# A QKV projection on one core: x's first row tiles spread over two DMA queues and handled in pairs

## The chip, the cores and the metric

The kernel runs on one core of a Trainium2 chip. The metric is the device time of one execution in microseconds. A core has TensorE (matmuls; the profile's PE, its weight loads PEld), VectorE (DVE), ScalarE (ACT), GpSimd (POOL) and SyncE (SP), which run their own instruction streams and wait for each other through semaphores. SP, ScalarE and GpSimd also issue DMAs; all of them run on the core's 16 DMA engines.

## The reference

```python
x:     16 x 512 x 768, fp32      w_qkv: 768 x 2304, fp32
qkv = np.matmul(x, w_qkv)
q, k, v = the three blocks of 768 columns
return np.stack([q, k, v], axis=0)
```

It is one matrix product of 8192 rows of x by 2304 columns, with 768 to sum over, whose columns are stored as three arrays.

## The kernel before, in words

The rows of x are taken in 32 pairs of two row tiles of 128 rows. The 768 values that are summed over are six k-slices of 128: slice j holds the rows p*6 + j of w. The columns of w are two blocks of 1024 (q = 0 and 1), each of two halves of 512 (c = 0 and 1), and a remainder of 256 columns.

Pairs 2 and up are computed with seven block products for each block of columns instead of eight, after Strassen and Winograd (`product`, `do`, lines 240 to 289), for which sums of blocks of x (`sums_x`) and of w (`sum_w`, L120) are needed. Pairs 0 and 1, the first four row tiles, are computed directly (`block`, L487): they need only casts to bf16, so that TensorE can work while w still arrives. All is in an order written out by hand, and each engine keeps the order of the program.

The head of the kernel, which the change touches, goes like this:

- **Loads.** On SP's queue: x's row tile 0, then tiles 1 to 3 (`load_row`, L169; 384 KB each, rows of 3 KB), then w slice by slice (`load_w`, L93): the first k-slice of the first 512 columns in two halves of 256 columns, then five slices of 256 KB, then six slices of the second 512 columns, then pair 2 of x in eight parts (L138) and larger blocks of w. On ScalarE's queue: two "touches", 128 bytes from each of 128 rows of w (L431) and of x's row tile 2 (L432); nothing reads them. Loads from SP and ScalarE take eight semaphores in turn, so each waits until the eighth load before it has landed.
- **GpSimd's queue.** A one-column copy of a slice of w (`hold`, L445) makes GpSimd wait until the sixth slice has landed; then it issues the DMAs of w's remainder (L450), and then it holds again, for pair 2 of x.
- **Row tiles.** Each row tile is cast to bf16, its first 384 columns by VectorE and the other 384 by ScalarE (`cast_row`, by `copy_halves`, L172 and L173). TensorE turns it with six 128x128 transposes (`turn_row`, L190) into two PSUM tiles of three. VectorE copies one of them to SBUF and ScalarE the other (L172, L173 again, with bf16 in PSUM as input). The program goes tile by tile: cast tile 0, turn tile 0, copy tile 0, cast tile 1, and so on, with the copy of a tile behind the cast of the next from tile 2 on.
- **Dummies.** `busy(n)` (L458) has TensorE multiply zeros, 8 times at the start and 2, 2 and 1 times between the transposes.
- **Casts of w.** `cast_j` casts a slice of w to bf16, on VectorE (L465) or ScalarE (L463).
- **First products.** `block` goes through the k-slices in order and adds each to the four row tiles' sums: for slice 0 the low 256 columns of tiles 0 to 2, their high 256 columns, and then tile 3 whole; then slices 1 to 5, four tiles each. A second call does the same for the second 512 columns, where the last three slices are taken tile by tile. Then come the remainder's products for those tiles (L334), and the products of pair 2.

`first`, the list of groups for slice 0, is this:

```python
    lo, hi = slice(0, half), slice(half, CB)
    first = [((0, ), range(3), lo), ((0, ), range(3), hi), ((0, ), (3, ))]
    first += [((j, ), range(4)) for j in range(1, KT)]
```

Code printed by the profile's line numbers:

Of the kernel before, what the change touches and what calls it, by code (L numbers as in the profile page):

```python
# [10 lines left out]
def kernel(  # L11
# [20 lines left out]
    nc = tc.nc  # L32
    P = 128
    G = 32
    B, T, H = x.shape
    M = B * T
    K = H
    N3 = w_qkv.shape[1]
    KT = K // P
    KH = KT // 2  # L40
# [3 lines left out]
    REM = N3 - 4 * CB  # L44
    Q_OFF = (0, 2 * CB + REM)
    R_OFF = 2 * CB
    fp32 = mybir.dt.float32
    f32r = mybir.dt.float32r
    bf16 = mybir.dt.bfloat16
# [4 lines left out]
    x_flat = x.rearrange("b t h -> (b t) h")  # L54
# [15 lines left out]
    m_pool = ctx.enter_context(tc.tile_pool(name="m", bufs=2))  # L70
    ps_pool = ctx.enter_context(tc.tile_pool(name="ps", bufs=8, space=bass.MemoryType.PSUM))
# [4 lines left out]
    eye = w_pool.tile([P, 176], bf16, name="eye")[:, :P]  # L76
    w_rem = [w_pool.tile([P, KH, REM], bf16, name="w_rem0"), None]

    b1 = [w_pool.tile([P, KT, CB], bf16, name=f"b1_{q}") for q in range(2)]
# [11 lines left out]
    def load_w(dst, j0, nj, off, cols):  # L91
        rows = w_qkv.rearrange("(p j) n -> p j n", j=KT)
        nc.sync.dma_start(dst, rows[:, j0:j0 + nj, off:off + cols])  # L93

    stage = {}
# [7 lines left out]
    def load_blocks(q, c):  # L103
        for h in range(2):
            if c == 0 and h == 0:
                t = st_first
            else:
                t = st_pool.tile([P, KH, CB], fp32, name="st1", tag="st")[:]
            load_w(t, h * KH, KH, Q_OFF[q] + c * CB, CB)
            stage[q, h, c] = t  # L110
# [11 lines left out]
    xin, xf, xb, sr = {}, {}, {}, {}  # L122
# [39 lines left out]

    def load_row(p, r):
        if r == 0:
            xin[p] = xin_pool.tile([P, 2, K], fp32, name="xin")
        row = (2 * p + r) * P
        nc.sync.dma_start(xin[p][:, r], x_flat[row:row + P, :])  # L169

    def copy_halves(dst, src):
        nc.vector.tensor_copy(out=dst[0], in_=src[0])  # L172
        nc.scalar.activation(dst[1], src[1], ident)  # L173
# [3 lines left out]
    def cast_row(p, r):  # L177
        if r == 0:
            xc[p] = s_pool.tile([P, 2, K], bf16, name="xc", tag="s")
        halves = (slice(0, K // 2), slice(K // 2, K))  # L180
        copy_halves([xc[p][:, r, n] for n in halves], [xin[p][:, r, n] for n in halves])

    def turn_row(p, r):
        if r == 0:
            xb[p] = xb_pool.tile([P, KT, 2 * P], bf16, name="xb", tag="xb")
        cols = xc[p][:, r, :].rearrange("m (p j) -> m j p", j=KT)
        ks = (slice(0, KH), slice(KH, KT))
        ps = [ps_pool.tile([P, KH, P], bf16, name="ps") for _ in ks]
        for j in range(KT):
            nc.tensor.transpose(ps[j // KH][:, j % KH, :], cols[:, j, :], eye)  # L190
        return lambda: copy_halves(
            [xb[p][:, n, r * P:(r + 1) * P] for n in ks], [t[:] for t in ps]
        )
# [6 lines left out]
    act, dve = nc.scalar, nc.vector  # L200
# [55 lines left out]
    def bank():  # L256
        return ps_pool.tile([P, CB], fp32, name="ps")
# [168 lines left out]
    ND = 2  # L426
    zero = xb_pool.tile([P, CB], bf16, name="zero", tag="xb")
    nc.vector.memset(zero[:], 0.0)
    load_row(0, 0)
    touch = m_pool.tile([P, 2, G], fp32, name="touch")  # L430
    nc.scalar.dma_start(touch[:, 0], w_qkv.rearrange("(p j) n -> p j n", j=KT)[:, 0, :G])  # L431
    nc.scalar.dma_start(touch[:, 1], x_flat[2 * P:3 * P, :G])  # L432
    nc.scalar.activation(tiny[:], zero[:, :1], ident)
    make_identity(nc, eye)
    load_row(0, 1)
    load_row(1, 0)
    load_row(1, 1)
    half = CB // 2
    load_slices(0, [(0, 1, 0, half), (0, 1, half, CB)] + [(j, 1, 0, CB) for j in range(1, KT)])
    load_slices(1, [(j, 1, 0, CB) for j in range(KT)])  # L440
# [2 lines left out]
    def hold(src):  # L443
        mark = m_pool.tile([P, 1], fp32, name="mark")
        nc.gpsimd.tensor_copy(out=mark[:], in_=src)  # L445

    hold(stage[0, 1, 0][:, KH - 1, :1])
    for h in range(2):
        rows = w_qkv.rearrange("(p j) n -> p j n", j=KT)[:, h * KH:(h + 1) * KH]
        nc.gpsimd.dma_start(w_rem[h][:], rows[:, :, R_OFF:R_OFF + REM])  # L450
    hold(xin[2][:, 0, :1])
    load_blocks(1, 0)

    def busy(n):

        ps = bank()
        for _ in range(n):
            nc.tensor.matmul(ps[:], zero[:, :P], zero[:], start=True, stop=True)  # L458

    def cast_j(q, c, w, j, eng=act, n=slice(0, CB)):  # L460
        src = stage[q, j // KH, c][:, j % KH, n]
        if eng is act:
            eng.activation(w[:, j, n], src, ident)  # L463
        else:
            eng.tensor_copy(out=w[:, j, n], in_=src)  # L465
# [54 lines left out]
        sums_x(p)  # L520

    lo, hi = slice(0, half), slice(half, CB)
    first = [((0, ), range(3), lo), ((0, ), range(3), hi), ((0, ), (3, ))]
    first += [((j, ), range(4)) for j in range(1, KT)]

    busy(8)
    cast_row(0, 0)
    turned = [turn_row(0, 0)]
    busy(2)
    turned[0]()  # L530
    cast_row(0, 1)
    turned.append(turn_row(0, 1))
    busy(2)
    cast_row(1, 0)
    turned[1]()
    turned.append(turn_row(1, 0))
    busy(1)
    cast_row(1, 1)
    turned[2]()
    cast_j(0, 0, b1[0], 0, dve, lo)  # L540
    turned.append(turn_row(1, 1))
    cast_j(0, 0, b1[0], 0, dve, hi)
    turned[3]()
    for j in range(1, KT):
        cast_j(0, 0, b1[0], j, dve)
    late0 = block(0, 0, b1[0], first)
# [165 lines left out]
```

## Time and profile before

| | |
|---|---|
| median of 3 runs | 360.48 us (360.26 to 360.60) |
| the profiled execution | 360.26 us |
| its span in the profile | 358.5 us |
| TensorE busy | 351.8 us (98%), 1760 instructions |
| VectorE, ScalarE, GpSimd busy | 65%, 52%, 50% |
| DMA | 107.73 MB, mean 301 GB/s over the span |

The span runs from the core's first instruction to its last; what lies around it, 1.76 us, is start and end of the execution. Times inside it count from the span's start. A matmul's end is modelled: the distance between the starts of two matmuls in a row is what one of them costs, 0.22 us for 512 columns when TensorE runs at its pace. In a row of the timeline, the figures are start, duration, engine, line, operation, output and input with shapes, and a count where several instructions in a row were merged; in brackets is the idle time before it and what ended it. "DMA to landing" counts from the start of the issue to the last semaphore update.

### The profile page before, as it was taken

The page shows a single profiled execution, that of the slowest core. Times are in us where ns is not written, and L with a number is a line of the kernel's source. Part 1 is how long each engine was busy: PE and PEld are TensorE (multiplying, and loading weights), DVE is VectorE, ACT ScalarE, POOL GpSimd, SP SyncE. Part 2 cuts the span into 40 slices and gives each one's busy share as a digit, 9 for nine tenths or more (in the row PEclk, how much of TensorE's full clock was granted, in tenths as well). Part 3 has the DMA queues.
Part 4 walks back from the last instruction along what each step waited for, and adds up shares of the span by engine and source line. Part 5 has one row for each costly group of instructions (what it writes and reads, how often), then busy time and mean ns, then how long its engine had stood idle before and what let it go on. Part 6 is the DMA issues. An engine that isn't in the chain of part 4 may idle for free.

```text
span 358.5 us, 5212 instructions
## 1 busy us (share of the span) xinstructions
PE 351.8 (98%) x1760; PEld 252.6 (70%) x1780; DVE 231.7 (65%) x245; ACT 185.5 (52%) x316; POOL 178.5 (50%) x187
## 2 busy tenths in 40 slices
PE   8999999999999999999999999999999999999995
PEld 4465577767768687786867768687776867768764
DVE  3789776878475675746676474676647577544643
ACT  5469644445545545454554545545454544545443
POOL 0223775582664717447372664717447371754420
PEclk9999999999999999999999999999999999999999
DMA  7998999999999898989989799898989989755767
GB/s 265 347 373 313 323 353 360 369 346 342 339 298 317 286 261 328 261 317 299 289 323 250 309 283 332 282 264 329 268 293 307 294 321 251 312 217 224 273 243 256
DMA packets 82106, 107.73 MB, mean 301 GB/s; under 512 B 5408, under 2 KB 62240, under 8 KB 82080
## 3 DMA queue, kind: packets, MB, share of 16 engines
q1 hardware_dynamic: 74288, 101.86, 86.1%
q10 hardware_dynamic: 6992, 5.15, 5.9%
q0 software_dynamic: 800, 0.39, 0.8%
q8 instruction: 14, 0.23, 0.3%
q14 instruction: 12, 0.10, 0.1%
HBM read 32.28 MB, written 75.50 MB: 301 GB/s over the span
## 4 chain that ended last, share of the span: by engine, by line
PE 93%; DMA 4%; ACT 1%; ACTq 1%; issue 0%
PE ps L251 78%; PE ps L306 11%; PE ps L487 4%; DMA st<-in_w_qkv_dram 3%; DMA touch<-in_x_dram 1%; PE ps L334 1%; ACT o L286 0%; ACTq L385 0%; ACT orem L399 0%; ACT both L463 0%; ACTq L431 0%; ACTq L401 0%; ACTq L399 0%
## 5 line engine op out<-in xcount | busy, mean ns | idle before, releaser
L251 PE MATMUL ps<-t,s 128*128 128x512 f32 x720 | 178.5, 396 | 0.0
L251 PEld LDWEIGHTS ps<-t,s 128*128 128x128 f32 x720 | 134.9, 188 | 29.8 <-ACT o L276 0.3
L154 DVE STREAM_TRANSPOSE xf<-xin 128x1536 f32<-128x1536 f32 (+1 forms) x33 | 91.2, 2767 | 2.5 <-DMA xin<-in_x_dram 2.5
L218 POOL TENSOR_TENSOR s<-xf 128x384 fp32r<-128x384 f32 x29 | 30.8, 1061 | 116.4 <-PE ps L251 115.0
L251 PE MATMUL ps<-b,xb 128*128 128x512 bf16 x342 | 81.7, 379 | 1.2
L283 DVE TENSOR_TENSOR o<-o,ps 128x512 f32<-128x512 f32 x58 | 39.7, 685 | 60.2 <-ACT o L282 60.2
L251 PEld LDWEIGHTS <-xb 128*128 128x128 bf16 x360 | 33.8, 98 | 36.9 <-issue 4.7
L273 DVE TENSOR_TENSOR o<-o,ps 128x512 f32<-128x512 f32 x60 | 39.0, 681 | 29.5 <-PE ps L251 22.4
L282 ACT ACTIVATE o<-ps 128x512 f32<-128x512 f32 x58 | 34.7, 598 | 44.2 <-PE ps L251 44.2
L276 ACT ACTIVATE o<-ps 128x512 f32<-128x512 f32 x60 | 36.0, 600 | 36.6 <-PE ps L251 34.0
L289 DVE TENSOR_TENSOR o<-o,ps 128x512 f32<-128x512 f32 x60 | 41.1, 687 | 20.7 <-PE ps L251 19.6
L260 ACT ACTIVATE o<-ps 128x512 f32<-128x512 f32 x60 | 35.7, 597 | 31.3 <-PE ps L251 18.3
L251 PE MATMUL ps<-b,s 128*128 128x512 f32 x180 | 50.4, 389 | 0.0
L198 POOL CAST xb<-xf 128x1536 bf16<-128x1536 f32 x28 | 41.0, 1464 | 16.7 <-DVE xf L154 16.7
L286 ACT ACTIVATE o<-ps 128x512 f32<-128x512 f32 x60 | 35.9, 598 | 24.3 <-PE ps L251 21.3
L306 PE MATMUL ps<-w_rem,xb 128*128 128x256 bf16 x360 | 44.6, 273 | 0.0
L306 PEld LDWEIGHTS <-xb 128*128 128x128 bf16 x360 | 34.9, 98 | 11.0 <-issue 1.1
L251 PEld LDWEIGHTS ps<-b,s 128*128 128x128 f32 x180 | 33.8, 188 | 7.1
L219 POOL TENSOR_TENSOR s<-s,xf 128x384 fp32r<-128x384 f32 x29 | 29.3, 1009 | 1.3
L220 POOL TENSOR_TENSOR s<-xf 128x384 fp32r<-128x384 f32 x29 | 29.3, 1009 | 0.0
L222 POOL TENSOR_TENSOR s<-xf,s 128x384 fp32r<-128x384 f32 x29 | 29.3, 1009 | 0.0
L323 ACT ACTIVATE orem<-ps 128x512 f32<-128x512 f32 x31 | 18.5, 597 | 20.7 <-PE ps L306 10.9
(47 smaller groups left out, 127.4 us busy)
## 6 DMA issues: line engine op xcount, KB each, us to landing
out_dram<-o SPq DMA_DIRECT2D x62, 768.0 KB, 4.5
xin<-in_x_dram SPq DMA_DIRECT2D x90, 192.0 KB, 6.5
out_dram<-o SPq DMA_DIRECT2D x65, 256.0 KB, 3.7
out_dram<-orem SPq DMA_DIRECT2D x31, 256.0 KB, 5.5
xin<-in_x_dram ACTq DMA_DIRECT2D x22, 192.0 KB, 6.9
st<-in_w_qkv_dram SPq DMA_DIRECT2D x11, 256.0 KB, 5.2
st<-in_w_qkv_dram SPq DMA_DIRECT2D x3, 768.0 KB, 10.0
xin<-in_x_dram SPq DMA_DIRECT2D x4, 384.0 KB, 4.5
```

The lines of the kernel that those rows point to most:

```text
L154: lambda g=g: nc.vector.transpose(turned[:, g:g + n], rows[:, g:g + n])
L198: nc.gpsimd.tensor_copy(out=xb[p][:], in_=t[:])
L218: 1: lambda g: g.tensor_tensor(s[:, 1], a21, a22, op=add),
L251: nc.tensor.matmul(ps[:], lhs[j], rhs[j], start=(start and j == 0), stop=(j == KH - 1), skip_group_check=True,)
L260: nc.scalar.activation(u.o[:, 0, :CB], u.x[:], ident)
L273: nc.vector.tensor_tensor(c11, c11, u.z[:], op=add)
L276: nc.scalar.activation(c12, u.x[:], ident)
L282: nc.scalar.activation(c22, u.x[:], ident)
L283: nc.vector.tensor_tensor(c22, c22, u.y[:], op=add)
L286: nc.scalar.activation(c21, u.x[:], ident)
L289: nc.vector.tensor_tensor(c12, c12, u.y[:], op=add)
L306: nc.tensor.matmul(ps, xb[p][:, j, r * P:(r + 1) * P], w_rem[j // KH][:, j % KH, :], start=(j == 0), stop=(j == KT - 1), skip_group_check= ...
```

## The change

1. x's row tiles 1 and 3 are loaded by ScalarE's queue instead of SP's, behind the touch of w. The touch of x is gone. SP's queue has tiles 0 and 2 and then w, as before.
2. The casts divide 448 columns to VectorE and 320 to ScalarE. The transposes go to PSUM tiles of four and two slices; VectorE copies the four, ScalarE the two.
3. The four tiles go in pairs: both casts of tiles 0 and 1, then all twelve transposes, then both copies; then the same for tiles 2 and 3. The dummies are 8 at the start and 2 behind the first twelve transposes.
4. Slice 0 of w: VectorE casts the low 256 columns, GpSimd the high 256. This cast stands ahead of GpSimd's first hold.
5. Slice 0 in `block`: low columns of tiles 0 and 1, high columns of tiles 0 and 1, then tiles 2 and 3 whole.

```diff
-    def load_row(p, r):
+    def load_row(p, r, eng=nc.sync):
...
-        nc.sync.dma_start(xin[p][:, r], x_flat[row:row + P, :])
+        eng.dma_start(xin[p][:, r], x_flat[row:row + P, :])
...
-        halves = (slice(0, K // 2), slice(K // 2, K))
+        halves = (slice(0, K * 7 // 12), slice(K * 7 // 12, K))
...
-        ks = (slice(0, KH), slice(KH, KT))
-        ps = [ps_pool.tile([P, KH, P], bf16, name="ps") for _ in ks]
-        for j in range(KT):
-            nc.tensor.transpose(ps[j // KH][:, j % KH, :], cols[:, j, :], eye)
+        ks = (slice(0, KT - 2), slice(KT - 2, KT))
+        ps = [ps_pool.tile([P, n.stop - n.start, P], bf16, name="ps") for n in ks]
+        for n, t in zip(ks, ps):
+            for j in range(n.start, n.stop):
+                nc.tensor.transpose(t[:, j - n.start, :], cols[:, j, :], eye)
...
-    load_row(0, 0)
-    touch = m_pool.tile([P, 2, G], fp32, name="touch")
-    nc.scalar.dma_start(touch[:, 0], w_qkv.rearrange("(p j) n -> p j n", j=KT)[:, 0, :G])
-    nc.scalar.dma_start(touch[:, 1], x_flat[2 * P:3 * P, :G])
+    touch = m_pool.tile([P, G], fp32, name="touch")
+    nc.scalar.dma_start(touch[:], w_qkv.rearrange("(p j) n -> p j n", j=KT)[:, 0, :G])
+    for p in range(2):
+        load_row(p, 0)
+        load_row(p, 1, nc.scalar)
     nc.scalar.activation(tiny[:], zero[:, :1], ident)
     make_identity(nc, eye)
-    load_row(0, 1)
-    load_row(1, 0)
-    load_row(1, 1)
...
-    first = [((0, ), range(3), lo), ((0, ), range(3), hi), ((0, ), (3, ))]
+    first = [((0, ), range(2), lo), ((0, ), range(2), hi), ((0, ), range(2, 4))]
...
     busy(8)
-    cast_row(0, 0)
-    turned = [turn_row(0, 0)]
+    for r in range(2):
+        cast_row(0, r)
+    turned = [turn_row(0, r) for r in range(2)]
     busy(2)
-    turned[0]()
-    cast_row(0, 1)
-    turned.append(turn_row(0, 1))
-    busy(2)
-    cast_row(1, 0)
-    turned[1]()
-    turned.append(turn_row(1, 0))
-    busy(1)
-    cast_row(1, 1)
-    turned[2]()
+    for f in turned:
+        f()
+    for r in range(2):
+        cast_row(1, r)
     cast_j(0, 0, b1[0], 0, dve, lo)
-    turned.append(turn_row(1, 1))
-    cast_j(0, 0, b1[0], 0, dve, hi)
-    turned[3]()
+    cast_j(0, 0, b1[0], 0, nc.gpsimd, hi)
+    hold(stage[0, 1, 0][:, KH - 1, :1])
...
+    hold(xin[2][:, 0, :1])
+    load_blocks(1, 0)
+    for r in range(2):
+        turn_row(1, r)()
```

The lines with the holds, w's remainder and `load_blocks(1, 0)` are moved down unchanged; SP issues the same DMAs behind the row tiles in the same order.

More of the change, by code (lines that the diff above doesn't have):

```diff
@@ L445, in hold @@
         nc.gpsimd.tensor_copy(out=mark[:], in_=src)
[L447 to L452, printed above, removed]
     def busy(n):
@@ L522 @@
     lo, hi = slice(0, half), slice(half, CB)
-    first = [((0, ), range(3), lo), ((0, ), range(3), hi), ((0, ), (3, ))]
+    first = [((0, ), range(2), lo), ((0, ), range(2), hi), ((0, ), range(2, 4))]
     first += [((j, ), range(4)) for j in range(1, KT)]
     busy(8)
-    cast_row(0, 0)
-    turned = [turn_row(0, 0)]
+    for r in range(2):
+        cast_row(0, r)
+    turned = [turn_row(0, r) for r in range(2)]
     busy(2)
-    turned[0]()
-    cast_row(0, 1)
-    turned.append(turn_row(0, 1))
-    busy(2)
-    cast_row(1, 0)
-    turned[1]()
-    turned.append(turn_row(1, 0))
-    busy(1)
-    cast_row(1, 1)
-    turned[2]()
-    cast_j(0, 0, b1[0], 0, dve, lo)
-    turned.append(turn_row(1, 1))
-    cast_j(0, 0, b1[0], 0, dve, hi)
-    turned[3]()
+    for f in turned:
+        f()
+    for r in range(2):
+        cast_row(1, r)
+    cast_j(0, 0, b1[0], 0, dve, lo)
+    cast_j(0, 0, b1[0], 0, nc.gpsimd, hi)
+    hold(stage[0, 1, 0][:, KH - 1, :1])
+    for h in range(2):
+        rows = w_qkv.rearrange("(p j) n -> p j n", j=KT)[:, h * KH:(h + 1) * KH]
+        nc.gpsimd.dma_start(w_rem[h][:], rows[:, :, R_OFF:R_OFF + REM])
+    hold(xin[2][:, 0, :1])
+    load_blocks(1, 0)
+    for r in range(2):
+        turn_row(1, r)()
     for j in range(1, KT):
```

## The prediction

> **What bounds the kernel now.** I read the page's first two parts and its chain, then the chain of waits in order of time, the timeline of the first 20 us by engine, the stretches of half a microsecond, and the DMA view of single stretches. The chain by engine (page), then its start in order of time (start, us, what):
>
> ```profile
> PE 93%; DMA 4%; ACT 1%; ACTq 1%; issue 0%
> ```
> ```profile
> 1.18 4.04 DMA touch<-in_x_dram
> ...
> 5.23 5.24 DMA st<-in_w_qkv_dram
> ...
> 10.48 6.09 DMA st<-in_w_qkv_dram
> ...
> 16.60 0.64 ACT both L463
> ...
> 17.28 2.32 PE ps L487 x10
> ```
>
> Up to 16.6 us the end is set by transfers, from 17.28 us to the last stores by TensorE without a real gap. So only the head can change, and a shift of TensorE's work there goes through to the end one for one. The last link of the head is the last 256 KB slice of w: it lands at 10.48 + 6.09 = 16.57, ScalarE casts it, TensorE takes it at 17.28. The timeline shows how close the race is (start, us, engine, line, operation; a release in brackets):
>
> ```profile
> 4.08 0.52 ACT L173 ACTIVATE xc<-xin 128x384 bf16<-128x384 f32 x1 [0.92 <-DMA xin<-in_x_dram]
> 6.49 0.84 PE L190 MATMUL ps<-eye,xc 128*128 128x128 bf16 x6
> 6.72 0.36 DVE L172 CAST xc<-xin 128x384 bf16<-128x384 f32 x1 [0.89 <-DMA xin<-in_x_dram]
> 7.60 0.50 PE L190 MATMUL ps<-eye,xc 128*128 128x128 bf16 x6
> 7.88 0.36 DVE L172 CAST xc<-xin 128x384 bf16<-128x384 f32 x1 [0.47 <-DMA xin<-in_x_dram]
> 8.46 0.54 PE L190 MATMUL ps<-eye,xc 128*128 128x128 bf16 x6
> 8.83 5.36 PE L487 MATMUL ps<-b,xb 128*128 128x256 bf16 x26
> 17.28 1.82 PEld L487 LDWEIGHTS <-xb 128*128 128x128 bf16 x9 [0.35 <-issue]
> ```
>
> Row tiles land at about 4.05, 5.05 (from the DMA view's 3.9 us after its issue at 1.18), 6.70 and 7.86. The first real product starts at 8.83. From there TensorE is dense; its only hole is before 17.28, where matmul starts stand 0.44 apart instead of 0.22: **0.22 us of slack**. A first product up to 0.22 late costs nothing; one that is early gains nothing unless the last slice of w is early too.
>
> **The change, part by part.**
>
> *Queues.* How do two queues share the engines? In the stretch from 2.5 to 3.0 us, when tile 0 runs on SP's queue (q1) beside the touches on ScalarE's (q10):
>
> ```profile
> q1 hardware_dynamic: 45, 0.14, 68.7%
> q10 hardware_dynamic: 48, 0.01, 7.5%
> ```
>
> Packet for packet. Each tile is 128 packets of 3 KB, eight for each of 16 engines, 0.97 us for a tile (64 such packets take 97.2% of 16 engines' half microsecond from 3.5 to 4.0: 121 ns each). So after the change the touch's packets pass beside tile 0, which still lands at 4.05; then tile 1 (ScalarE's queue) alternates with tile 2 (SP's), and both end when all of both have passed. Tile 1, now at 5.05, comes at the earliest one tile later, 5.05 + 0.97 - 0.1 = **5.9** (the touch of x is gone: 8 packets of about 13 ns per engine), at the latest with tile 2's present time, 6.70 - 0.1 = **6.6**. I take **6.4**: nearer the late end, since tile 2's 1.65 us (0.97 would do) holds a loss that its engines would share with tile 1. Two stretches show that loss (core's stretch, busy us of each engine, clock, DMA share, GB/s):
>
> ```profile
> 3.50:4.00 0.50, 0.50 (x3) 0.15 (x1) 0.00 (x0) 0.00 (x0) 0.00 (x0) 1.00 1.03 402
> 5.50:6.00 0.50, 0.50 (x2) 0.00 (x0) 0.34 (x2) 0.47 (x2) 0.00 (x0) 1.00 0.81 252
> ```
>
> Tile 3 then alternates with w's two 1 KB-row halves and lands between 7.5 and 8.1; now 7.86. The bytes in all are the same, so w's slices, the last one too, come only the touch's 0.1 us earlier.
>
> [...]
>
> *Pairs.* VectorE's and ScalarE's order becomes cast 0, cast 1, copy 0, copy 1, cast 2, cast 3, (w's half), copies 2 and 3. Both engines now stand at cast 1 until tile 1 lands, with copy 0, copy 1 and the casts of tiles 2 and 3 queued behind, and TensorE waits for those. Durations: DVE casts 0.36 for 384 columns, 0.43 for 512 (L465), so 0.40 for 448; ACT 0.52 for 384 and 0.65 for 512 (L463), so 0.46 for 320; DVE copies 0.36 for 384, so 0.43 for 512; ACT copies 0.49, so 0.36 for 256. Instructions in a row start about 0.1 before the one ahead ends on ACT (four evictions of L477 in 2.06), 0.08 on DVE. From tile 1 at 6.40:
>
> - ACT cast 1 6.42 to 6.88; six transposes from 6.93, at the slow spacing (0.107, as at 6.49, and 0.31 for the last to end): the fourth, which VectorE's copy needs, ends at 7.56, the sixth at 7.78;
> - ACT copy 1 7.80 to 8.16, cast 2 to 8.52, cast 3 8.42 to 8.88. VectorE: copy 1 7.58 to 8.01, cast 2 to 8.33, cast 3 to 8.65, half of w to 8.85, so ACT is last;
> - transposes of tile 3 from 8.93; the first product 0.37 later (8.46 to 8.83 now): **9.30**.
>
> That is 0.47 later than now. The slack takes 0.22; the last slice's 0.1 us earlier landing is then no bound. **Cost: 0.25.** With tile 1 at 5.9 the product starts at 8.8 and costs nothing; at 6.6, 0.45.
>
> *GpSimd's half cast* (128x256) is in no row. Below, its 128x1 copy (0.18, 0.44 beside VectorE); above, its 128x384 cast (0.87). I take 0.44: w's second half lands at 8.5 (3.09 + 5.5, less 0.1), so it ends at 8.9, and is wanted at 9.5, two half matmuls after the first. Hidden; at 0.87 still. If VectorE held it off until 9.7, 0.2 would show: I add 0.05. VectorE loses one 0.28 cast, off the path. The holds and w_rem's DMAs behind this cast on GpSimd wait for a slice that lands at 11.8, so they don't move. ScalarE's queue issues three DMAs for two (0.42 more); its table load then ends at about 3.6, before 4.05: nothing. Three dummy matmuls fewer: only the clock can feel them (below).
>
> Sum: 0.25 + 0.05 = **+0.3 us**. The profiled execution took 360.26 (span 358.5 and 1.76 around it), 0.22 under the median 360.48. On the median: **360.8**.
>
> **The rivals.**
>
> *A, slower: the clock comes late.* The first eight matmuls stand 0.43 apart, later ones 0.22; transposes 0.107 at 6.49 and 0.055 at 7.60. The change of pace fell near 7.2, after TensorE had worked since 1.19 with dummies (L458) in the gaps. After the change TensorE has nothing between tile 0's transposes (end 5.3) and 6.93. If that hole puts the change of pace off past the first product, tile 3's transposes take 0.27 more and every microsecond until the change does half its work. Ends: nothing, and, if it needs again the 6.0 us from 1.19 to 7.2, counted from 6.93, (12.9 - 9.6)/2 = 1.65. I take 0.7 + 0.27, under the middle, as the work before the hole may count: 360.8 + 0.9 = **361.7**. It decides when the change of pace falls after 9.3.
>
> [...]
>
> *B, faster: two queues hide the loss.* Against 402 GB/s, the five stretches from 4.5 to 7.0 (330, 356, 252, 315, 324) miss 0.22 MB, 0.54 us; the ramp from 2.5 to 3.5 (289, 379) 0.17; the touch 0.1: 0.8 at most. Then tile 1 is at 5.7, the product at 8.6, w's last slice at 15.8, and both bounds let the end move by 0.5 (the product's start) to 0.8 (if transposes keep the fast pace too, the product starts 0.3 earlier): **359.7** at full size. Against it: every engine serves both queues in turn, so its stall holds both. What is late next would be x's third pair: its rounding ends at 23.9 and is used at 24.0.
>
> *C, nothing:* tile 1 by 6.1, the slack swallows the rest, w's last slice 0.1 earlier: 360.48 - 0.1 = **360.4**. That is also the answer if the change doesn't do what it says, the queues only sharing.
>
> **How the numbers follow.** Forecast 0.36, A 0.34 (what decides it, the length of work that the clock asks for, shows once in this trace), B 0.18, C 0.12. A measurement tells 0.2% from no change, 0.72 us: faster is under 359.76, slower over 361.20. Faster: B at nearly full size, two thirds of it: 0.12. Slower: nearly all of A (0.33) and the forecast's upper end (tile 1 at 6.6 and a late GpSimd, 0.08): 0.41. Within: 0.47. Range: 359.8 to 361.9, which leaves out those 0.12 below and the part of A past 1.4 us, 0.08. The forecast's own range is 360.4 to 361.2.
>
> **What would show it.** In the profile after: the first product's start (9.3), the cast of tile 1 released by its DMA at 6.4 on both engines, the hole before 17.28 gone (dense from 9.3), the last slice of w landing at about 16.5. A: matmuls 0.43 apart after 9.3. B: slices of w landing over 0.4 earlier. C: the hole still there. Wrong altogether if tile 1 lands beside tile 0 near 5, if GpSimd's cast ends after 9.7, or if anything after 17.28 loses TensorE time.

## The result, and the profile after

The changed kernel takes 361.77 us (median of 22 runs, 360.41 to 363.19) against 360.43 us for the kernel before, run beside it (22 runs, 359.80 to 362.46). The ratio is 1.0035, with a 95% interval of 1.0024 to 1.0046: slower by 1.3 us. That lies inside the range, near its upper end and at rival A's 361.7. The forecast itself, 360.8, was 1 us short.

| profiled execution | before | after |
|---|---|---|
| time | 360.26 | 362.00 |
| span | 358.48 | 359.85 |
| outside the span | 1.78 | 2.15 |
| row tile 1 landed | 5.05 | 6.52 |
| row tile 3 landed | 7.86 | 7.76 |
| first product starts | 8.83 | 9.72 |
| last slice of w landed | 16.58 | 16.60 |
| second block's 15th matmul | 17.28 | 18.51 |

The chain of waits of the changed kernel at its start (start, us, what) has changed its kind. The transfers of w are gone from it; one row tile and then TensorE's own work make it up:

```profile
1.18 5.34 DMA xin<-in_x_dram
...
6.54 0.48 ACT xc L173
...
7.09 0.52 PE ps L191 x6
7.61 0.85 PE ps L450 x2
8.45 1.47 PE ps L191 x12
9.92 3.35 PE ps L479 x15
...
13.33 7.50 PE ps L479 x34
```

The first piece is tile 1: issued at 1.18 on ScalarE's queue, landed at 6.52 (tile 2, on SP's queue beside it, landed at 6.36). The timeline of the changed kernel around it (start, duration, engine, line, what; the idle time before in brackets):

```profile
4.60 0.52 PE L191 MATMUL ps<-eye,xc 128*128 128x128 bf16 x6
6.54 0.39 DVE L172 CAST xc<-xin 128x448 bf16<-128x448 f32 x1 [2.10 <-DMA xin<-in_x_dram]
6.54 0.47 ACT L173 ACTIVATE xc<-xin 128x320 bf16<-128x320 f32 x1 [2.02 <-DMA xin<-in_x_dram]
6.85 0.42 DVE L172 COPY xb<-ps 128x512 bf16<-128x512 bf16 x1
7.09 0.52 PE L191 MATMUL ps<-eye,xc 128*128 128x128 bf16 x6 [1.97 <-ACT xc L173]
7.45 1.01 PE L450 MATMUL ps<-zero 128*128 128x512 bf16 x2
8.05 0.46 POOL L457 CAST b<-st 128x256 bf16<-128x256 f32 x1 [6.75 <-DMA st<-in_w_qkv_dram]
8.44 1.48 PE L191 MATMUL ps<-eye,xc 128*128 128x128 bf16 x12
9.72 0.84 PE L479 MATMUL ps<-b,xb 128*128 128x256 bf16 x3
```

Both engines stand 2 us before the cast of tile 1, and tile 0's copy, whose transposes ended before 5.2, starts only at 6.85 behind it. TensorE has a hole of 2 us. What follows is the part that the forecast left to a rival: six transposes take 0.52 at 4.60 and at 7.09, but twelve take 1.48 at 8.44. Three stretches of the same profile show why (stretch, length, busy us of each engine with instruction counts, granted clock, DMA share, GB/s):

```profile
4.10:7.40 3.30, 1.24 (x14) 0.73 (x13) 1.07 (x3) 1.17 (x3) 0.00 (x0) 1.00 1.03 393
7.50:10.80 3.30, 3.30 (x21) 2.06 (x19) 2.90 (x9) 1.87 (x5) 0.46 (x1) 0.50 1.04 380
11.00:14.00 3.00, 2.95 (x15) 1.35 (x15) 2.01 (x6) 0.00 (x0) 1.91 (x3) 1.00 0.98 346
```

The clock had come up by 4.1, earlier than in the profile before (7.2). After a stretch in which TensorE was busy for 1.24 of 3.30 us it was halved, from 7.5 to 10.9, over tile 2's and 3's transposes and the first products.

### The profile page after: what moved, and what is told of

Same layout as the page of the kernel before. It is cut to its first block, busy times and chain, and to the rows that moved or that the text cites. A ratio compares the mean times of both kernels' runs of the same rounds, so it can differ in the third digit from the quotient of the medians.

```text
span 359.9 us, 5203 instructions
## 1 busy us (share of the span) xinstructions
PE 351.4 (98%) x1756; PEld 252.2 (70%) x1776; DVE 230.4 (64%) x244; ACT 185.1 (51%) x316; POOL 177.3 (49%) x188
## 4 chain that ended last, share of the span: by engine, by line
PE 96%; DMA 1%; ACT 1%; ACTq 1%; issue 1%
PE ps L252 78%; PE ps L307 11%; PE ps L479 6%; DMA xin<-in_x_dram 1%; PE ps L335 1%; PE ps L191 1%; ACT o L287 0%; ACTq L386 0%; PE ps L450 0%; ACT orem L400 0%; ACT xc L173 0%; ACTq L431 0%; ACTq L402 0%; ACTq L400 0%
```

## The experiments

Each was timed beside the kernel before. All times are us; the ratio is to that kernel.

### The hole filled

```diff
-    turned = [turn_row(0, r) for r in range(2)]
+    turned = [turn_row(0, 0)]
+    busy(5)
+    turned.append(turn_row(0, 1))
     busy(2)
```

> The changed kernel with five more dummy matmuls between the transposes of row tiles 0 and 1, so that TensorE's hole of 2 us (5.1 to 7.1) is mostly filled. Theory K (the hole makes the clock fall back, which costs tile 3's transposes 0.3 us and the first products some 0.6 us): first product at 9.4, matmuls 0.22 apart from there, profile's span about 0.9 us under the changed kernel's 359.9, median about 361.0. Theory W alone (only the wait for tile 1 costs; the pace does not matter): no change, 361.8.

Median 361.11 (before: 360.27), ratio 1.0031 (1.0019 to 1.0043). The clock was whole from 3.9 on and the first product came at 8.97, so the half pace was indeed gone; but the span of this execution was 359.8, no shorter. In it something else held the end, as TensorE's weight loads show:

```profile
17.32 0.31 PEld L479 LDWEIGHTS <-xb 128*128 128x128 bf16 x2 [0.66 <-issue]
18.10 0.10 PEld L479 LDWEIGHTS <-xb 128*128 128x128 bf16 x1 [0.47 <-issue]
```

TensorE waited twice before the last products of w's second 512 columns, whose last two slices landed at 16.53 and 17.40 (before: 15.45 and 16.58). But the profiled execution is one of the two long ones of the seven: the other five have spans of 358.8 to 359.1, where the changed kernel's 22 have a median of 359.6. So filling the hole shortened the median span by some 0.7 us, near what theory K says. The clock that each execution lists, its mean over the span, says the same. A stretch of 3.4 us at half pace takes 1.7 of 359 us from it, which makes 0.995. The changed kernel lists 0.994 or 0.995 in nine of 22 executions; this kernel and the next one, both with the hole filled, in none of 19, and the kernel before in none of the 99 beside the experiments.

### The filling, and a later start of w's remainder

```diff
-    hold(stage[0, 1, 0][:, KH - 1, :1])
+    hold(stage[0, 0, 1][:, KH - 1, :1])
```

on top of the filling.

> The changed kernel with the five filling dummies, and GpSimd's first hold on the ninth slice of w instead of the sixth, so that the DMAs of w's remainder start about 2 us later. With the filling alone the first product came at 8.97 at full pace, and then TensorE waited 1.0 us for the last two slices (16.53 and 17.40). Theory D (the remainder's many small packets slow the slices): last slice at 16.6 or before, no wait of over 0.3 us before the second block's last products, span 358.7 to 359.0, median 360.7. Rival (the slices are late by stalls of their own, from 10 to 13 us): last slice still after 17.0, span over 359.5; or the remainder is now late for its own products, and the wait stands at 19.4 instead.

The last slice landed at 16.45 and that wait was gone; span 358.9. That doesn't show the remainder's DMAs to be the cause: the changed kernel has the early hold too, and its last slice landed at 16.60; and over all executions the median spans of the two kernels with the hole filled are alike, 358.9 and 358.85. The prediction's own chain can be checked here, with tile 1 late (6.50) and the clock whole from 6.9 on:

```profile
5.22 2.06 PE L450 MATMUL ps<-zero 128*128 128x512 bf16 x5
7.12 0.50 PE L191 MATMUL ps<-eye,xc 128*128 128x128 bf16 x6
7.45 0.59 PE L450 MATMUL ps<-zero 128*128 128x512 bf16 x2
8.45 0.98 PE L191 MATMUL ps<-eye,xc 128*128 128x128 bf16 x12 [0.40 <-ACT xc L173]
9.26 1.28 PE L479 MATMUL ps<-b,xb 128*128 128x256 bf16 x7
```

The twelve transposes take 0.98 with a wait of 0.40 before them, instead of 1.48, and the first product starts at 9.26; 9.30 was predicted. In the three profiles with both edits and a whole clock by then, the first product comes 2.66 to 2.76 us after tile 1 (8.53 after 5.87, 8.97 after 6.24, 9.26 after 6.50); the prediction's steps add up to 2.90. The span is 0.43 over that of before. The median is 361.01 against 360.14, ratio 1.0025 (1.0012 to 1.0037), 0.3 over what was expected; most of the rest is outside the span (2.15; below).

### The pair order with the old queues

```diff
-    for p in range(2):
-        load_row(p, 0)
-        load_row(p, 1, nc.scalar)
+    load_row(0, 0)
...
+    nc.scalar.dma_start(touch[:, 1], x_flat[2 * P:3 * P, :G])
...
+    load_row(0, 1)
+    load_row(1, 0)
+    load_row(1, 1)
```

on the changed kernel, so that its loads are those of the kernel before.

> The changed kernel with its row tiles and both touches loaded as before (all four tiles on SP's queue). Theory W + K (the harm comes from tile 1 landing at 6.5 instead of 5.05, behind which the pair order makes VectorE and ScalarE wait): tile 1 lands at 5.05, TensorE has no hole over 0.7 us, first product at 8.8 to 8.9, median 360.3 to 360.6. Rival P (the pair order by itself costs, wherever the tiles come from): first product after 9.2, median over 361.

Tile 1 landed at 5.08, the first product started at 8.84, the span is 358.63. So in this profile the pair order by itself delays nothing. The median is higher than expected, 361.02 against 360.27, ratio 1.0026 (1.0013 to 1.0039): 2.13 outside the span, and a spread from 360.33 to 362.60; the median of the eleven spans is 358.9, against 358.5 before. The longest execution lists a clock of 0.995, the second longest (362.23) 0.998, and no profile shows either; where these 0.4 us come from stays open.

### The queues with the old order

The mirror image, on the kernel before:

```diff
-    load_row(0, 0)
...
-    nc.scalar.dma_start(touch[:, 1], x_flat[2 * P:3 * P, :G])
+    for p in range(2):
+        load_row(p, 0)
+        load_row(p, 1, nc.scalar)
...
-    load_row(0, 1)
-    load_row(1, 0)
-    load_row(1, 1)
```

> The kernel before with only the queues changed: tiles 1 and 3 on ScalarE's queue behind the touch of w, no touch of x; tile-by-tile order, dummies and splits as before. Tile 1 lands at 6.5 as in the changed kernel. Theory W (late tile 1 hurts only because the pair order queues copy 0, copy 1 and the next casts behind it): copy 0 runs at 5.2, first product at 8.8 to 9.1, median 360.3 to 360.8. Rival Q (the queues alone are the loss): first product at 9.3 or later and TensorE's hole drops the clock, median over 361.3.

Tile 1 landed at 6.29. VectorE's and TensorE's rows of this kernel:

```profile
5.14 0.36 DVE L172 COPY xb<-ps 128x384 bf16<-128x384 bf16 x1 [0.80 <-PE ps L190]
...
6.31 0.63 DVE L172 CAST xc<-xin 128x384 bf16<-128x384 f32 x2 [0.81 <-DMA xin<-in_x_dram]
...
8.42 0.54 PE L190 MATMUL ps<-eye,xc 128*128 128x128 bf16 x6
8.80 0.38 PE L485 MATMUL ps<-b,xb 128*128 128x256 bf16 x2
```

Copy 0 runs at 5.14 without waiting for tile 1, tiles 1 and 2 are cast together at 6.31, and the first product starts at 8.80. Median 360.63 against 360.27, ratio 1.0011 (1.0000 to 1.0023). The first product starts at 8.83 with neither edit, at 8.80 with the queues and at 8.84 with the pairs alone. With both it starts at 8.53, 8.97, 9.26 and 9.72, in the order in which tile 1 lands (5.87, 6.24, 6.50, 6.52). There it is the late tile, behind which the pair order queues everything.

The late tile has a price without the pairs too. The chain of waits of the kernel with the queues alone starts with it:

```profile
1.18 5.11 DMA xin<-in_x_dram
...
6.31 0.53 ACT xc L173
...
6.89 0.54 PE ps L190 x6
```

Its first product comes 1.27 us after tile 3, the last to land (7.53); in the kernel before it was 0.97 (8.83 after 7.86). Tile 3 came 0.33 earlier, and that hid it. Over all executions the spans of this kernel have a median of 358.9, 0.4 over the kernel before, as those of the pairs alone do. How the wait divides between the two edits is therefore not settled.

### The clock by itself

```diff
     turned = [turn_row(0, 0)]
-    busy(2)
     turned[0]()
...
-    busy(2)
     cast_row(1, 0)
...
-    busy(1)
     cast_row(1, 1)
```

> The kernel before without the five dummy matmuls between the transposes (the eight at the start stay); nothing else. Nothing that the first products need comes later. Theory K (holes in TensorE's work keep or pull the clock down in part of the executions): times spread over 1 us or more, median 0.3 to 1.0 us over before; in a profile with the low clock at 8.8, transposes 0.107 and first products 0.43 apart. Rival (the dummies do nothing, and the changed kernel's loss is waiting alone): 360.1 to 360.6, spread as before.

Five dummy matmuls less, nothing else, on the kernel before: median 361.04 against 360.14, ratio 1.0028 (1.0015 to 1.0041), and the twelve executions spread from 359.80 to 362.44. TensorE in the profiled one:

```profile
4.77 0.84 PE L190 MATMUL ps<-eye,xc 128*128 128x128 bf16 x6
6.60 1.48 PE L190 MATMUL ps<-eye,xc 128*128 128x128 bf16 x12 [0.99 <-ACT xc L173]
8.61 0.84 PE L190 MATMUL ps<-eye,xc 128*128 128x128 bf16 x6 [0.53 <-ACT xc L173]
9.25 5.12 PE L487 MATMUL ps<-b,xb 128*128 128x256 bf16 x23
```

All transposes run at the slow pace (0.84 for six), and the pace rises only at 10.1. From 3.3 to 6.6 TensorE was busy for 2.31 us here. In the kernel with only the queues changed, which has the dummies, it was busy for 2.98 us of the same stretch, and the pace rose at 6.6. Four of the twelve executions list a clock of 0.995. The dummies matter although nothing reads what they compute.

### The other parts of the change

The kernel before with the new splits, groups and GpSimd's cast, but its own queues and order:

```diff
-        halves = (slice(0, K // 2), slice(K // 2, K))
+        halves = (slice(0, K * 7 // 12), slice(K * 7 // 12, K))
...
-        ks = (slice(0, KH), slice(KH, KT))
+        ks = (slice(0, KT - 2), slice(KT - 2, KT))
...
-    first = [((0, ), range(3), lo), ((0, ), range(3), hi), ((0, ), (3, ))]
+    first = [((0, ), range(2), lo), ((0, ), range(2), hi), ((0, ), range(2, 4))]
...
-    cast_j(0, 0, b1[0], 0, dve, hi)
-    turned[3]()
+    cast_j(0, 0, b1[0], 0, nc.gpsimd, hi)
+    hold(stage[0, 1, 0][:, KH - 1, :1])
...
+    turned[3]()
```

> The kernel before with only the remaining parts of the change: casts split 448 to 320, copies four to two, GpSimd's cast of the upper half of w's first slice ahead of its hold, slice 0 in groups of two tiles. Queues and tile-by-tile order as before. All theories: nothing, 360.2 to 360.6, first product within 0.1 us of 8.83. Rival G (GpSimd's cast is late or slows VectorE): a gap before the upper half's matmuls, up to 0.3 us more.

Median 360.78 against 360.27, ratio 1.0016 (1.0007 to 1.0025): not nothing. In the profile tile 3 landed at 8.19, and the first product at 9.19 followed it; but the time outside the span was 2.16, which no row of the profile explains. So two parts were run alone. The first is GpSimd's cast:

```diff
-    cast_j(0, 0, b1[0], 0, dve, hi)
+    cast_j(0, 0, b1[0], 0, nc.gpsimd, hi)
+    hold(stage[0, 1, 0][:, KH - 1, :1])
...
     turned[3]()
```

The hold, the DMAs of w's remainder and `load_blocks(1, 0)` move behind it, as in the change.

> The kernel before with one part of the change: GpSimd casts the upper half of w's first slice, ahead of its hold. Kernels with the change's remaining parts took 2.15 us outside the profile's span, the kernel before and the one with the queues alone 1.78. Theory O1 (one of the remaining parts adds this 0.37, and it is GpSimd's cast): time minus span 2.15, median 360.6 to 360.9. Theory O2 (it is not this part): 1.78, median 360.1 to 360.5. The first product is at 8.8 in both.

Median 360.64 against 360.14, ratio 1.0008 (0.9999 to 1.0018); 2.16 outside the span. The second is the splits of casts and copies:

```diff
-        halves = (slice(0, K // 2), slice(K // 2, K))
+        halves = (slice(0, K * 7 // 12), slice(K * 7 // 12, K))
...
-        ks = (slice(0, KH), slice(KH, KT))
+        ks = (slice(0, KT - 2), slice(KT - 2, KT))
```

> The kernel before with one part of the change: casts split 448 to 320 and PSUM tiles of four and two slices. Theory O1 (GpSimd's cast adds the 0.37 us outside the span): time minus span 1.78, median 360.1 to 360.5. Theory O2 (the splits add it): 2.15, median 360.6 to 360.9. Rival E (the splits themselves are slow): tile 3's transposes, now 0.60 us after its landing, later by 0.1 or more.

Median 359.94 against 360.14, ratio 0.9999 (0.9989 to 1.0009); 1.77 outside the span; tile 3's transposes 0.57 behind its landing, before 0.60. So the extra time comes with GpSimd's cast, and the changed kernel was run with VectorE in its place:

```diff
-    cast_j(0, 0, b1[0], 0, nc.gpsimd, hi)
+    cast_j(0, 0, b1[0], 0, dve, hi)
```

> The changed kernel with the upper half of w's first slice cast by VectorE again. Theory O1 (GpSimd's cast adds 0.37 us outside the span): time minus span 1.78 instead of 2.15; VectorE's 0.28 us more delays copies 2 and 3 but not the first product, so the median falls by 0.1 to 0.4, to about 361.4, with the spread of the changed kernel, since the hole and the clock stay. Rival (that time belongs to the pairs or the moved lines): 2.15 stays, and the median.

1.79 outside the span, median 361.29 against 360.35, ratio 1.0020 (1.0007 to 1.0033). Its twelve executions fall into two groups with nothing between them, four from 359.99 to 360.46 and eight from 361.24 to 362.17. The profiled one (360.31) kept its clock, tile 1 had landed at 5.87, and the first product started at 8.53. Of the eight long ones only two list a clock of 0.994 or 0.995. A pace that rises late doesn't lower that figure (0.999 in the profile without the dummies, where it rose at 10.1), so whether it was the clock that lengthened the other six is not known. Is it any further instruction on GpSimd?

```diff
+    hold(tiny[:])
     hold(stage[0, 1, 0][:, KH - 1, :1])
```

> The kernel before with one more one-column copy on GpSimd, of a value that is there by 4 us, ahead of its first hold. Theory N (any further GpSimd instruction there brings the 0.37 us outside the span): time minus span 2.15, median 360.5. Theory O1 in its narrow form (it is the cast of w whose result TensorE waits for): 1.78, median as before, 360.2.

It isn't: 1.78, median 360.16 against 360.35, ratio 0.9993 (0.9982 to 1.0004).

### The touch of x, and the parts that looked best

```diff
-    nc.scalar.dma_start(touch[:, 1], x_flat[2 * P:3 * P, :G])
```

> The kernel before without the touch of x. With two queues w's slices 1 to 5 landed 0.2 to 0.6 us earlier than in the kernel before. Theory T (that comes from the missing touch, which also lets each load of w wait on one load fewer): slice 1 at 8.6 to 9.0. Theory B2 (it comes from the second queue): slice 1 at 9.1 or later, tile 3 at 7.8 or later, median 360.2 to 360.6.

The kernel before without that touch: 360.40 against 360.35, ratio 1.0000 (0.9990 to 1.0010). w's slice 1 landed at 8.72 and tile 3 at 7.38, so the earlier slices of the changed kernel (8.63) need no second queue. This is one profile; with the touch and one queue slice 1 landed between 8.93 and 9.56 (seven kernels), with two queues between 8.19 and 8.74 (six).

The last kernel is the one with the queues changed alone, plus the splits, plus this:

```diff
-    busy(2)
+    busy(4)
     turned[0]()
```

> What the runs favour, together: tiles 1 and 3 on ScalarE's queue, splits of 448 to 320 and four to two, tile-by-tile order, two more dummies ahead of tile 1's transposes to keep the clock, VectorE for all of w's first slice. Theory W + K: first product at 8.5 to 8.7 (tile 3 lands at 7.55), no half pace in most executions, time minus span 1.78, last slice at 16.4: 359.7 to 360.1, 0.1 to 0.4 under the kernel before. Rival (the last slices are later for stalls, as in two of the kernels with two queues): a wait before the second block's last products, 360.3 or more.

Median 360.52 against 360.35, ratio 1.0007 (0.9997 to 1.0017). The clock held and the spread was small (all but one from 359.93 to 360.79), but in the profiled execution tile 3 landed at 7.95, tile 1 at 6.80, and the first product started at 9.26. No version was faster than the kernel before by more than its interval.

## Why the prediction was right or wrong, point by point

- **What bounds the kernel: right.** Nearly all that moved inside the span moved in the head: the second block's 15th matmul came 1.23 later, TensorE's last product 1.30, and the span is 1.37 longer.
- **The queues: right.** Tile 1 at 6.52 (6.4, between 5.9 and 6.6), tile 2 at 6.36 and so nearly together with it, tile 3 at 7.76 (7.5 to 8.1). In the other profiles with both edits tile 1 landed between 5.87 and 6.50, over nearly all of the range. The last slice of w came at 16.60, not 0.1 earlier. Slices 1 to 5 did come about 0.6 earlier (slice 1 at 8.63 for 9.21) and lost that again between 10 and 13 us, where DMA moved 346 GB/s from 11 to 14 against 399 to 410 before; some packets took 0.3 to 0.8 us there. Why is open.
- **The pairs: right in kind, and near in size.** 9.26 with the clock whole, for 9.30. With the hole filled the spans have a median of 358.9, 0.4 to 0.5 over the kernel before (358.5 and 358.4), for the 0.3 of the sum.
- **Rival B: no.** Its sign, slices over 0.4 earlier, was there for slices 1 to 5, but the gain didn't reach the last slice. Nor is it shown to come from the second queue: without the touch of x, one queue brings w's slice 1 about as early (8.72) as two do (8.19 to 8.74).
- **The step that failed: "transposes of tile 3 from 8.93; the first product 0.37 later".** These 0.37 are the whole pace; the clock was left out of the sum and made a rival with a chance of 0.34. In the profiled execution the slow transposes cost 0.46 (9.72 less 9.26), and the half pace from 9.72 to 10.9 half of 1.18, 0.59. With the wait of 0.43 (9.26 less 8.83) and less the slack of 0.22 this gives 1.26, near the 1.23 measured at that matmul. How often it happens: nine of the 22 executions list a clock of 0.994 or 0.995; they took 361.95 to 362.54, median 362.31. The other thirteen have a median of 361.17. 1.14 lies between them, against the 0.9 that rival A was priced at. So A's price was nearly right, and nine in 22 is not far from its chance of 0.34. What the forecast had wrong is that it made the half pace a thing that either comes or stays away, while one kernel has executions with it and without. Its mechanism was half right: the clock wasn't late, it had come up at 4.1 and was taken back.
- **That 361.77 meets rival A's 361.7 is in part luck.** The thirteen's 361.17 is the forecast's 360.8 and the 0.37 outside the span that the sum had at nothing (below). The nine have the fall of the clock on top, and the median of all 22 falls between the two groups, at two executions that list 0.999. One execution took 363.19 with a listed clock of 1.0; the record doesn't show why.
- **The fall of the clock, as measured.** It fell after a stretch with TensorE 1.24 of 3.30 us busy (4.1 to 7.4), and the half pace lasted 3.4 us, from 7.5 to 10.9. The sum had neither.
- **GpSimd's cast: wrong in kind.** It took 0.46 and was hidden (0.44 taken), but 0.37 came outside the span, which the sum had held constant at 1.76. Five kernels with the cast show it beside the changed one (2.13 to 2.16); the eight without it, the kernel before included, show 1.77 to 1.88. Over all executions of the experiments it is 2.09 or more with the cast and 1.89 or less without. That the cast brings it is shown by taking it out and putting it in; by what way is open.

Together in the profiled execution: 1.23 up to the second block's 15th matmul, 0.37 outside the span, and 0.14 behind that matmul, not traced, of 1.74.

## What to carry to other kernels

A transfer moved to a second queue isn't simply earlier. Here it shared the engines with its neighbours and came 1.5 us later (6.52 for 5.05), so look which transfer becomes later, and what each engine has queued in program order behind the wait for it. TensorE's idle time off the critical path can have a price of its own when a dense stretch follows: here five dummy matmuls were worth 0.9 us (361.04 without them, 360.14 with), so when an edit opens a hole, put the clock into the sum and not beside it. One profile is one execution: set its span beside those of the others before reading a cause from it. And compare the time outside the span too; an edit can add there what no row shows.

## What the runs showed of the hardware that was not expected

- Where the clock changes differs between executions. In each of the 14 traces the long stretch at the whole clock is 348.16, 351.57 or 354.99 us, lengths that stand 3.41 apart: 351.57 in the profile before, and 348.16 in the changed kernel's, with 3.41 at the whole and 3.41 at half the clock ahead of it. The work that TensorE is given up to 4.4 us is the same eight dummies everywhere, yet the clock came up at 3.9 in the kernel with the hole filled, at 4.1 in the changed kernel and at 7.2 in the kernel before; without the dummies between the transposes it came up at 10.1. It fell after 1.24 of 3.30 us busy (4.1 to 7.4, above) and held in the changed kernel with VectorE's cast after 1.68 of 3.30 (below), and in six further profiles after 1.90 or more:

```profile
4.90:8.20 3.30, 1.68 (x20) 1.06 (x19) 2.04 (x7) 1.84 (x5) 0.00 (x0) 1.00 1.04 394
```

- The clock column can't be trusted ahead of its first change: it says 1.00 in the profile before from the start, where matmuls stand 0.43 apart. The pace of the matmuls tells it.
- A row tile's landing spreads by over half a microsecond between kernels with the same loads ahead of it: tile 3 in SP's order, with both touches, between 7.55 and 8.19. One profile can't settle an effect of that size in the head.
